# Forty fixed steps of attention on TensorE, two-bank logits rows and gated products over five heads

## The chip, the cores and the metric

The kernel runs on one core of one Trainium2 chip. A core has five engines with instruction streams of their own: TensorE (PE in the profile, with its weight loads shown apart as PEld), VectorE (DVE), ScalarE (ACT), GpSimd (POOL) and SyncE (SP, which here only issues DMA transfers). They share an on-chip memory of 128 partitions and an accumulator memory, PSUM, of eight banks of 128 x 512 float32 into which TensorE writes. The engines run side by side and wait for each other through semaphores; each executes its own stream in order.

The metric is the device time of one execution in microseconds, as the median over runs. Lower is better.

## The reference, cut to what matters

One layer of a decoder block over 1024 tokens of width 1024, in float32. Attention with 8 heads of 64 and a gated mixer of 512 channels stand side by side, and a convolutional feed-forward network follows.

```python
xn = rmsnorm(h, norm_mix_g)
proj = xn @ w_in                       # q, k, v, u, vg, forget gates
# attention, per head, per block of 128 queries
c = cumsum(log_sigmoid(forget + b_forget))
logits = q @ k.T * Dh ** -0.5 + c_q - c_k
p = softmax(where(causal, logits, -inf))
att = p @ v
# gated mixer
sg = u * (tril(w_spatial) @ rmsnorm(vg) + b_spatial)
h = h + concat([att, sg]) @ w_out
h = h + conv_ffn(rmsnorm(h), ...)      # 1024 -> 2 x 2816 -> 1024
out = rmsnorm(h, norm_final_g)
```

The change concerns the attention of the eight heads and the product of the gated mixer's result with its half of `w_out`, which the kernel computes during attention.

## The kernel before, in words

Matrix products are made in a split format: each operand is held as a rounded high part and the remainder, a low part, so that one product becomes two or three matmuls (high x high, high x low, low x high). The high part is a copy that rounds, the low part a subtraction.

The program has stages: the input projection; the gated mixer, whose result is turned by transposes on TensorE into `sgT` (`turn_sg`); attention; the out-projection of the attention half (`wmm`, lines 963 to 965) with the second normalisation; the feed-forward network (lines 1054 and 1306); the final normalisation. A planner orders the instructions of each engine from their dependencies and the order in which the program lists them; ordering edges that carry no semaphore are put in by hand with `after(...)`.

**Attention** is `att_head(h)`, called for h = 0 to 7. It loads q and k of the head in split form (tiles A, B, B2), and `ck`, a row of cumulative gates broadcast over the partitions. Then it runs over four pairs i = 0 to 3 of query blocks, two blocks j = 2i and 2i+1 of 128 queries each:

- Logits row j covers the keys 0 to (j+1) x 128, in one or two pieces of at most 512 columns, each in a PSUM bank of its own (tag "s", four banks). Each piece is two matmuls (L783, L784).
- The causal mask is written by POOL (`affine_select`, L776): it reads `ck` and writes the masked columns of the last piece to the row's own tile.
- DVE reduces each piece (L786): it adds the gates, stores the result and takes the running minimum; where a row has two pieces, the second starts from the minimum of the first. Each is followed by a read of the accumulator. A head has 12 of these.
- ACT takes the exponential of the whole row and sums it (L789).
- For each pair of key blocks (k0) a group follows: TensorE transposes the probabilities (L812) into a bank of tag "b", ACT copies the high part (L813, tile `pt`), DVE subtracts the low part (L814), and TensorE multiplies with the values (L822) into another bank. A head has 10 groups.
- After the pairs 1 and 3, ACT and DVE evacuate the finished half (L828, L829) to `attF`.

`row_tail(h)` inverts the row sums and transposes them (L730), and sends them through memory to be spread over the columns; it is called in the next head at i = 0. `pair_end` multiplies a finished pair of heads by these and splits the product in high and low (L744, L747, L750), on POOL for the first three pairs, behind the last select of pair i = 2 in head 2, 4 or 6. `wo_load` brings the attention half of `w_out`; POOL splits it (L873, L874).

**The fills.** `sg_out` is a generator: each step computes one 128 x 512 tile of the gated mixer's product with its half of `w_out`, in 12 matmuls (L851 to L853), an addition of the input on DVE (L854) and a store. There are 16 steps. The list `FILLS` says how many steps are listed behind each pair i of each head: one and two in turn, so that all 16 are listed by the third pair of head 2. The weights of the second half of the columns are split on ACT and POOL (L153, L159) ahead of the ninth step.

PSUM is one pool for the whole program: four banks of tag "s" and four of tag "b" (transposes, values, fills, row tails).

Of the kernel before, what the change touches and what calls it, by code (L numbers as in the profile page):

```python
# [8 lines left out]
F32 = mybir.dt.float32  # L9
# [3 lines left out]
ALU = mybir.AluOpType  # L13
# [6 lines left out]
FILLS = [1, 2] * 10 + [2] + [0] * 11  # L20
# [44 lines left out]
def block_kernel(ctx: ExitStack, tc: tile.TileContext, xT, xtok, wuv, wv, wqk, wf, cpk, bfv,  # L65
# [12 lines left out]
    psa = ctx.enter_context(tc.tile_pool(name="psa", bufs=4, space=bass.MemoryType.PSUM))  # L78
# [645 lines left out]
    def row_tail(h, ex):  # L724
# [5 lines left out]
        pe.transpose(ptr[0:8, 0:P], rs, ident)  # L730
        c = act.copy(rt, ptr[0:8, 0:P])
        if ex is not None:
            after(tc, c, ex)
# [4 lines left out]
    def pair_end(p, sel):  # L738

        attT[p] = sb("A" if p < 2 else "G", [P, 2, 1024], F32R)  # L740
        f = attF[p]
        for o in (slice(0, 512), slice(512, 1024)):
            eng = pool if p < 3 else dve
            m = eng.tensor_tensor(out=f[:, 0, o], in0=f[:, 0, o], in1=f[:, 1, o], op=ALU.mult)  # L744
            if p < 3:
                after(tc, m, sel)
                pool.tensor_copy(attT[p][:, 0, o], f[:, 0, o])  # L747
            else:
                act.copy(attT[p][:, 0, o], f[:, 0, o])
            eng.tensor_tensor(out=attT[p][:, 1, o], in0=f[:, 0, o], in1=f32(attT[p][:, 0, o]), op=ALU.subtract)  # L750

    def att_head(h, order=(0, 1, 2, 3)):
        p, hh = h // 2, h % 2
        ab, nb = sb("x1", [P, 2, 1024], F32R), sb("x2", [P, 2, 1024], F32R)
        A, B, ck, B2 = ab[:, 0, :], ab[:, 1, :], f32(nb[:, 0, :]), nb[:, 1, :]
        sp.dma_start(out=f32(A), in_=qd[h].rearrange("s d t -> (s d) t"))
        sp.dma_start(out=f32(B), in_=kd[h].rearrange("s d t -> (s d) t"))
        sp.dma_start(out=ck, in_=ncd[h:h + 1, :].to_broadcast((P, 1024)))
        sp.dma_start(out=f32(B2[0:64, :]), in_=kd[h, 1])
        loads[h] = sp.dma_start(out=f32(B2[64:128, :]), in_=kd[h, 0])  # L760
        if hh == 0:
            attF[p] = sb("H", [P, 2, 1024])
        rs = sml.tile([P, 8], F32, tag="rs", name=nm("rs"))
        rows[h] = rs
        po = None
        for i in order:
            w1, w2 = (2 * i + 1) * P, (2 * i + 2) * P
            tp = sb(TTAG[i][h % 2], [P, w1 + w2])
            tj = (tp[:, 0:w1], tp[:, w1:w1 + w2])
            for jj in range(2):  # L770
                j = 2 * i + jj
                n = (j + 1) * P
                qs = slice(j * P, (j + 1) * P)
                t = tj[jj]
                c0 = (j // 4) * 512
                sel = pool.affine_select(out=t[:, c0:n], in_=ck[:, c0:n], pattern=[[-1, n - c0]], compare_op=ALU.is_ge,  # L776
                                   fill=BIG, base=j * P - c0, channel_multiplier=1)
                mn = sml.tile([P, 2], F32, tag="mn", name=nm("mn"))
                lo_ = lim[:, 0:1]
                for c in range(0, n, 512):  # L780
                    e = min(n, c + 512)
                    ps = sbank()
                    pe.matmul(ps[:, 0:e - c], A[:, qs], B[:, c:e], start=True, stop=False)  # L783
                    pe.matmul(ps[:, 0:e - c], A[:, qs], B2[:, c:e], start=False, stop=True)  # L784
                    m = mn[:, c // 512:c // 512 + 1]
                    dve.tensor_tensor_reduce(out=t[:, c:e], in0=ps[:, 0:e - c], in1=(t if c == c0 else ck)[:, c:e], scale=1.0,  # L786
                                             scalar=lo_, op0=ALU.add, op1=ALU.min, accum_out=m)
                    lo_ = m
                ex = act.activation(t, t, AF.Exp, bias=lo_, scale=-1.0, accum_out=rs[:, j:j + 1])  # L789
                exs.append(ex)  # L790
            sels[h].append(sel)
            if h == 7 and i == 3:
                wo_load((2, 3))
                row_tail(7, None)
            if h > 0 and i == 0:
                row_tail(h - 1, ex)
            if h in (2, 4, 6) and i == 2:
                pair_end(p - 1, sel)
            for _ in range(FILL[4 * h + list(order).index(i)]):
                next(filler, None)  # L800
            if i % 2 == 0:
                po = bank()
            oc = (i % 2) * 256
            for k0 in range(0, 2 * i + 2, 2):
                pt = sb("pt", [P, 2, 512], F32R)
                ptr = bank()
                diag = k0 == 2 * i
                blocks = [(k0, 0, 0), (k0, 1, 128)] + ([(k0 + 1, 1, 256)] if diag else
                                                      [(k0 + 1, 0, 256), (k0 + 1, 1, 384)])
                w = 384 if diag else 512  # L810
                for k, jj, c in blocks:
                    pe.transpose(ptr[:, c:c + P], tj[jj][:, k * P:(k + 1) * P], ident)  # L812
                act.copy(pt[:, 0, 0:w], ptr[:, 0:w])  # L813
                dve.tensor_tensor(out=pt[:, 1, 0:w], in0=ptr[:, 0:w], in1=f32(pt[:, 0, 0:w]), op=ALU.subtract)  # L814
                for k in (k0, k0 + 1):
                    lhs = V[k // 2][:, k % 2, h, :, :].rearrange("p s d -> p (s d)")
                    half = k == 2 * i + 1
                    o = (k - k0) * 256
                    n = 128 if half else 256
                    oo = oc + (128 if half else 0)  # L820
                    for s in range(2):
                        pe.matmul(po[:, oo:oo + n], lhs, pt[:, s, o:o + n], start=(k == 0 and s == 0),  # L822
                                  stop=(s == 1 and half))
            if i % 2 == 1:
                hf = i // 2
                o = slice(hf * 512, hf * 512 + 512)
                r = slice(hh * 64, hh * 64 + 64)
                act.copy(attF[p][r, 0, o], po[64:128, :])  # L828
                dve.tensor_tensor(out=attF[p][r, 0, o], in0=po[0:64, :], in1=attF[p][r, 0, o], op=ALU.add)  # L829
        if h == 7:  # L830
            pair_end(3, None)

    def sg_out():
        for hf in range(2):
            o = slice(hf * 512, hf * 512 + 512)
            whs = []
            for kp in range(2):
                wr = sb("raw", [P, 2, 512])
                sp.dma_start(out=wr, in_=wos[hf, kp])
                for j in range(2):  # L840
                    w = sb("whl", [P, 2, 512], F32R)
                    split_w(wr[:, j, :], (w[:, 0], w[:, 1]), "act", "pool")
                    whs.append(w)
            for tt in range(8):
                ts_ = slice(tt * P, (tt + 1) * P)
                hs = sb("raw", [P, 512])
                sp.dma_start(out=hs, in_=xtok[ts_, o])
                ps = fbank()
                for k in range(4):
                    w = whs[k]  # L850
                    pe.matmul(ps, sgT[k][:, 0, ts_], w[:, 0, :], start=(k == 0), stop=False)  # L851
                    pe.matmul(ps, sgT[k][:, 0, ts_], w[:, 1, :], start=False, stop=False)  # L852
                    pe.matmul(ps, sgT[k][:, 1, ts_], w[:, 0, :], start=False, stop=(k == 3))  # L853
                dve.tensor_tensor(out=hs, in0=ps, in1=hs, op=ALU.add)  # L854
                sp.dma_start(out=hpd[tt, :, o], in_=hs)
                yield
# [5 lines left out]
    def wo_load(ks):  # L862
        for k in ks:
            wr = sb("raw", [P, 1024])
            after(tc, sp.dma_start(out=wr, in_=woa[k]), loads[4])
# [5 lines left out]
            for hf in range(2):  # L871
                src = wr[:, hf * 512:hf * 512 + 512]
                after(tc, pool.tensor_copy(w[hf][:, 0], src), sels[5][2 * k + hf] if k < 2 else sels[7][3])  # L873
# [3 lines left out]
    for h in range(8):  # L877
        if h == 7:
            for _ in filler:
                pass  # L880
            wo_load((0, 1))
        att_head(h)
# [7 lines left out]
    early.release()  # L890
    upl = tc.alloc_tile_pool(name="upl", bufs=1, reuse_waits="tile")
# [513 lines left out]
    raws.release()  # L1405

# [45 lines left out]
```

## Time and profile before

| | us |
|---|---|
| median of 3 runs | 1077.31 (1076.47 to 1077.58) |
| profiled execution | 1076.71 |
| its span in the trace | 1075.0 |
| first fill matmul | 225.00 |
| last fill matmul | 304.28 |
| last value matmul of head 7 | 390.8 |
| first matmul of the feed-forward network | 437.36 |

The profile is one execution: a page with busy time by engine, the span in 40 slices, the chain of work that ended last, and groups of instructions by line; the trace behind it answers for any window. A row of a group reads: line, engine, operation, output <- inputs, shape, count | busy us, mean ns of one | idle time of the engine just before these, and what ended it. A matmul's record is longer than the time until the next one starts, so records overlap. Line numbers here are those of the kernel before unless the text says otherwise.

### The profile page before, as it was taken

How to read it: one execution, taken by the hardware profiler on the slowest of the kernel's cores; microseconds unless marked ns; L12 is line 12 of the kernel's file. 1: busy time of each engine (PE TensorE's matmuls, PEld its weight loads, DVE VectorE, ACT ScalarE, POOL GpSimd, SP SyncE). 2: the span in 40 equal slices, each digit the busy share in tenths (PEclk: the TensorE clock that was granted, in tenths of full speed). 3: DMA queues.
4: the chain of work that ended last, by engine and by line, in shares of the span. 5: the costliest groups of instructions: out<-in, count | busy, mean ns of one | idle time of the engine just before them, and what ended most of it. 6: DMA issues, size and time to landing. Idle time of an engine off the chain costs nothing.

```text
span 1075.0 us, 14470 instructions
## 1 busy us (share of the span) xinstructions
PE 1062.7 (99%) x5013; PEld 876.6 (82%) x5013; DVE 892.4 (83%) x1363; ACT 568.0 (53%) x984; POOL 249.5 (23%) x223
## 2 busy tenths in 40 slices
PE   9999999999999999999999999999999999999997
PEld 7888788787888888878888888888888888888886
DVE  5985798775689969999899999989988776898774
ACT  6666644554468855764444444444444444454653
POOL 0002134233046541054333333333322000000000
PEclk9999999999999999999999999999999999999999
DMA  9242267937557445132244513222331899433442
GB/s 345 90 140 96 74 156 218 278 118 224 188 166 207 129 137 185 72 117 98 98 137 164 170 69 127 98 98 98 108 118 45 289 326 317 125 95 97 141 125 96
DMA packets 66297, 160.80 MB, mean 150 GB/s; under 512 B 7976, under 2 KB 8240, under 8 KB 66224
## 3 DMA queue, kind: packets, MB, share of 16 engines
q1 hardware_dynamic: 65792, 159.32, 45.4%
q8 instruction: 39, 0.64, 0.2%
q10 hardware_dynamic: 432, 0.57, 0.1%
q14 instruction: 34, 0.28, 0.1%
HBM read 117.06 MB, written 42.80 MB: 149 GB/s over the span
## 4 chain that ended last, share of the span: by engine, by line
PE 77%; ACT 2%; DVE 2%; issue 1%; POOL 0%; DMA 0%; DVEq 0%; ACTq 0%
PE k L1306 19%; PE qa L1054 11%; PE qc L1054 11%; PE qd L1054 11%; PE qb L1054 5%; PE pb L822 3%; PE pb L812 2%; PE ps L257 2%; PE pf L852 1%; PE pf L853 1%; PE pf L851 1%; PE ps L783 1%; PE ps L784 1%; PE pb L964 1%; PE pb L963 1%; PE pb L965 1%
## 5 line engine op out<-in xcount | busy, mean ns | idle before, releaser
L1306 PE MATMUL k<-whb,wha 128*128 128x512 f32 x924 | 209.7, 389 | 0.0
L1306 PEld LDWEIGHTS k<-whb,wha 128*128 128x128 f32 x924 | 173.3, 188 | 36.2 <-DVE wha L159 0.2
L1054 PE MATMUL qc<-xT,whb 128*128 128x512 f32 x540 | 129.8, 389 | 0.0
L1054 PE MATMUL qa<-xB,wha 128*128 128x512 f32 x528 | 127.2, 390 | 0.0
L1054 PEld LDWEIGHTS qc<-xT,whb 128*128 128x128 f32 x540 | 101.3, 188 | 21.2 <-ACT whb L153 0.2
L1054 PEld LDWEIGHTS qa<-xB,wha 128*128 128x128 f32 x528 | 98.8, 188 | 20.8 <-DVE wha L159 0.4
L153 ACT CAST wha<-sg 128x512 fp32r<-128x512 f32 x77 | 47.8, 622 | 96.9 <-PE k L1306 85.8
L153 ACT CAST whb<-sg 128x512 fp32r<-128x512 f32 x82 | 50.5, 617 | 86.6 <-PE qc L1054 67.0
L159 DVE TENSOR_TENSOR wha<-sg,wha 128x512 fp32r<-128x512 f32 x77 | 52.7, 687 | 41.1 <-ACT wha L153 41.0
L1054 PE MATMUL qd<-xB,whb 128*128 128x512 f32 x264 | 63.9, 389 | 0.5 <-DVE h L1173 0.5
L1054 PE MATMUL qd<-xT,whb 128*128 128x512 f32 x264 | 63.6, 389 | 0.0
L159 DVE TENSOR_TENSOR whb<-sg,whb 128x512 fp32r<-128x512 f32 x82 | 58.2, 710 | 4.4 <-ACT whb L153 4.3
L941 POOL TENSOR_TENSOR sg<-raw 128x512 f32<-128x512 f32 x20 | 30.7, 1535 | 134.0 <-DVE whb L159 75.7
L813 ACT CAST pt<-pb 128x512 fp32r<-128x512 f32 (+1 forms) x80 | 40.6, 543 | 38.5 <-PE pb L812 37.4
L1054 PE MATMUL qb<-xT,whb 128*128 128x512 f32 x252 | 60.9, 389 | 0.0
L822 PE MATMUL pb<-pt,V 128*128 128x256 f32 (+1 forms) x320 | 58.7, 298 | 1.6 <-ACT pt L813 1.2
L1054 PEld LDWEIGHTS qd<-xB,whb 128*128 128x128 f32 x264 | 49.5, 188 | 11.2 <-issue 0.9
L1054 PEld LDWEIGHTS qd<-xT,whb 128*128 128x128 f32 x264 | 49.6, 188 | 10.3
L822 PEld LDWEIGHTS pb<-pt,V 128*128 128x128 f32 x320 | 46.8, 188 | 13.5 <-ACT pt L813 8.9
L1054 PEld LDWEIGHTS qb<-xT,whb 128*128 128x128 f32 x252 | 47.3, 188 | 9.8
L814 DVE TENSOR_TENSOR pt<-pb,pt 128x512 fp32r<-128x512 f32 (+1 forms) x80 | 48.1, 632 | 8.0 <-ACT pt L813 7.4
L944 POOL TENSOR_TENSOR sg<-sg,raw 128x512 f32<-128x512 f32 x20 | 33.3, 1666 | 64.6 <-DVE whb L159 64.6
(399 smaller groups left out, 2306.9 us busy)
## 6 DMA issues: line engine op xcount, KB each, us to landing
raw<-wup SPq DMA_DIRECT2D x44, 512.0 KB, 3.5
sg<-hx SPq DMA_DIRECT2D x77, 256.0 KB, 2.8
hx<-hs SPq DMA_DIRECT2D x44, 256.0 KB, 3.7
hx<-ca SPq DMA_DIRECT2D x35, 256.0 KB, 2.0
xT<-wdn SPq DMA_DIRECT2D x28, 256.0 KB, 4.1
raw<-wqk SPq DMA_DIRECT2D x8, 512.0 KB, 4.7
qd<-G SPq DMA_DIRECT2D x16, 256.0 KB, 3.9
kd<-G SPq DMA_DIRECT2D x16, 256.0 KB, 3.3
```

The lines of the kernel that those rows point to most:

```text
L153: act.copy(h, src)
L159: return eng.tensor_tensor(out=l, in0=src, in1=f32(h), op=ALU.subtract)
L257: pe.matmul(banks[m], xs(n, xi, k)[:, ms], w[:, wi, :], start=(first and k == 0 and c == 0), stop=(k == 3 and c == 2), skip_group_check=True)
L783: pe.matmul(ps[:, 0:e - c], A[:, qs], B[:, c:e], start=True, stop=False)
L812: pe.transpose(ptr[:, c:c + P], tj[jj][:, k * P:(k + 1) * P], ident)
L813: act.copy(pt[:, 0, 0:w], ptr[:, 0:w])
L814: dve.tensor_tensor(out=pt[:, 1, 0:w], in0=ptr[:, 0:w], in1=f32(pt[:, 0, 0:w]), op=ALU.subtract)
L822: pe.matmul(po[:, oo:oo + n], lhs, pt[:, s, o:o + n], start=(k == 0 and s == 0), stop=(s == 1 and half))
L941: pool.tensor_tensor(out=s[0], in0=a21, in1=a22, op=ALU.add)
L944: pool.tensor_tensor(out=s[3], in0=s[1], in1=a12, op=ALU.add)
L1054: pe.matmul(ps, w[:, wi, ks], xb[:, xi, k, :], start=(first and n == 0), stop=(n == 11), skip_group_check=True)
L1306: pe.matmul(banks[bk + m], xh[:, xi, ms], wh[:, wi, :], start=(first and p_ == 0 and n == 0), stop=(p_ == NP - 1 and n == 2), skip_group_c ...
```

## The change

Attention is written anew as a sequence that fixes the order of every TensorE instruction of the stage (`seq` chains each to the one before).

- There are 40 steps, five for each head, each with two of the head's ten groups, pairs i in the order 3, 2, 1, 0. `turn_p` (transposes, cast, low part) of the next step is issued ahead of `values` of this one.
- The logits of head h+1 are issued during head h, behind the values of a step: rows 7; 6; 5; 4 and 3; 2, 1 and 0. Those of head 0 come first, in a prologue.
- A logits row lies in one tile of 1024 columns, two neighbouring banks (tag "L", two such tiles). DVE reduces the whole row in one instruction (L797 of the changed file), 8 per head.
- The mask is written in place: POOL's select (L789) changes the 128 columns of the diagonal block in `ck` itself, one per row, from row 7 down.
- A value group multiplies first the two high parts, then the two low parts.
- `row_tail(h)` comes in step 1 of head h. `pair_half` (one half of a pair's product) stands in step 2 of heads 2, 4 and 6, both halves, on POOL behind the select of row 6 of the next head.
- The fills: one step each after rows 4, 2 and 0 of the prologue, then after steps 0, 2 and 4 of heads 0, 2 and 4 and steps 1 and 3 of heads 1 and 3. The second half's weights are loaded at the seventh step and split behind the eighth.
- All four parts of the attention half of `w_out` are loaded behind head 6's loads; POOL splits two behind selects of head 6 (which fall in head 5) and two behind select 4 of head 7 (which falls in head 6). The changed lines are L897 and L898.
- PSUM is taken as three pools in turn (before, during and after attention).

```diff
-FILLS = [1, 2] * 10 + [2] + [0] * 11
+FILLS = {(-1, j): 1 for j in (4, 2, 0)} | {(h, s): 1 for h in range(5) for s in ((0, 2, 4), (1, 3))[h % 2]}
...
+    def pair_half(p, o):
...
+        m = eng.tensor_tensor(out=f[:, 0, o], in0=f[:, 0, o], in1=f[:, 1, o], op=ALU.mult)
+        if p < 3:
+            after(tc, m, sels[2 * p + 3][1])
+            pool.tensor_copy(attT[p][:, 0, o], f[:, 0, o])
...
+        eng.tensor_tensor(out=attT[p][:, 1, o], in0=f[:, 0, o], in1=f32(attT[p][:, 0, o]), op=ALU.subtract)
+    psa.release()
+    psa = tc.alloc_tile_pool(name="psb", bufs=4, space=bass.MemoryType.PSUM, reuse_waits="tile")
+    def seq(m):
+        if order:
+            after(tc, m, order[0])
+        order[:] = [m]
+    cks, b2s = sb("x2", [P, 2, 1024]), sb("x2", [P, 2, 1024], F32R)
...
+    def logits(h, j):
...
+        sels[h].append(pool.affine_select(out=ck[:, qs], in_=ck[:, qs], pattern=[[-1, P]], compare_op=ALU.is_ge,
+                                          fill=BIG, base=0, channel_multiplier=1))
+        mn = sml.tile([P, 1], F32, tag="mn", name=nm("mn"))
+        ps = psa.tile([P, 1024], F32, tag="L", bufs=2, name=nm("pl"))
+        for c in range(0, n, 512):
+            e = min(n, c + 512)
+            seq(pe.matmul(ps[:, c:e], A[:, qs], B[:, c:e], start=True, stop=False))
+            seq(pe.matmul(ps[:, c:e], A[:, qs], B2[:, c:e], start=False, stop=True))
+        dve.tensor_tensor_reduce(out=t, in0=ps[:, 0:n], in1=ck[:, 0:n], scale=1.0, scalar=lim[:, 0:1],
+                                 op0=ALU.add, op1=ALU.min, accum_out=mn)
+        exs.append(act.activation(t, t, AF.Exp, bias=mn, scale=-1.0, accum_out=rows[h][:, j:j + 1]))
+    def turn_p(g):
...
+        for k, jj, c in blocks:
+            seq(pe.transpose(ptr[:, c:c + P], tj[jj][:, k * P:(k + 1) * P], ident))
+        act.copy(pt[:, 0, 0:w], ptr[:, 0:w])
+        dve.tensor_tensor(out=pt[:, 1, 0:w], in0=ptr[:, 0:w], in1=f32(pt[:, 0, 0:w]), op=ALU.subtract)
+        return pt
+    def values(g, pt):
...
+        for s in range(2):
+            for k in (k0, k0 + 1):
...
+                seq(pe.matmul(po[0][:, oo:oo + n], lhs, pt[:, s, o:o + n], start=(k == 0 and s == 0),
+                              stop=(s == 1 and half)))
...
-            after(tc, sp.dma_start(out=wr, in_=woa[k]), loads[4])
+            after(tc, sp.dma_start(out=wr, in_=woa[k]), loads[6])
...
-                after(tc, pool.tensor_copy(w[hf][:, 0], src), sels[5][2 * k + hf] if k < 2 else sels[7][3])
+                after(tc, pool.tensor_copy(w[hf][:, 0], src), sels[6][2 * k + hf] if k < 2 else sels[7][3])
...
+    STEPS = [[(h, i, 2 * c) for i in (3, 2, 1, 0) for c in range(i + 1)] for h in range(8)]
+    STEPS = [s[n:n + 2] for s in STEPS for n in range(0, 10, 2)]
+    NEXT = ((7,), (6,), (5,), (4, 3), (2, 1, 0))
...
+    for j in range(7, -1, -1):
+        logits(0, j)
+        fill((-1, j))
+    turned = [turn_p(g) for g in STEPS[0]]
+    for n, step in enumerate(STEPS):
+        h, s = n // 5, n % 5
+        if s == 0 and h < 6:
+            head_loads(h + 2)
+        if h == 7 and s == 0:
...
+            wo_load((0, 1))
+            wo_load((2, 3))
+        if s == 1:
...
+            row_tail(h)
+        if h in (2, 4, 6) and s == 2:
+            for o in (slice(0, 512), slice(512, 1024)):
+                pair_half(h // 2 - 1, o)
+        now, turned = turned, [turn_p(g) for g in STEPS[n + 1]] if n + 1 < len(STEPS) else []
+        for g, pt in zip(step, now):
+            values(g, pt)
+        if h < 7:
+            for j in NEXT[s]:
+                logits(h + 1, j)
+        fill((h, s))
...
     early.release()
+    psa.release()
+    psa = tc.alloc_tile_pool(name="psc", bufs=4, space=bass.MemoryType.PSUM, reuse_waits="tile")
```

More of the change, by code (lines that the diff above doesn't have):

```diff
@@ L77, in block_kernel @@
     FTAG, FB, BB = FCFG
-    psa = ctx.enter_context(tc.tile_pool(name="psa", bufs=4, space=bass.MemoryType.PSUM))
+    psa = tc.alloc_tile_pool(name="psa", bufs=4, space=bass.MemoryType.PSUM)
     uid = [0]
@@ L729, in row_tail @@
         dve.reciprocal(rs, rs)
[L730 to L733, printed above, removed]
+        seq(pe.transpose(ptr[0:8, 0:P], rs, ident))
+        act.copy(rt, ptr[0:8, 0:P])
         act.dma_start(out=rsd[h], in_=rt)
@@ L736, in row_tail @@
                      in_=rsd[h].rearrange("a b -> (a b)").unsqueeze(0).to_broadcast((64, 1024)))
-    def pair_end(p, sel):
-        attT[p] = sb("A" if p < 2 else "G", [P, 2, 1024], F32R)
+    def pair_half(p, o):
+        if attT[p] is None:
+            attT[p] = sb("A" if p < 2 else "G", [P, 2, 1024], F32R)
         f = attF[p]
[L742 to L831, printed above, removed]
@@ new lines, in block_kernel, with head_loads @@
+    order = []
+    def seq(m):
[3 more added lines that the diff above has]
+    cks, b2s = sb("x2", [P, 2, 1024]), sb("x2", [P, 2, 1024], F32R)
+    abs_, places = [None] * 8, {}
+    def head_loads(h):
+        ab = sb("x1", [P, 2, 1024], F32R)
+        abs_[h] = ab
+        hh = h % 2
+        sp.dma_start(out=f32(ab[:, 0, :]), in_=qd[h].rearrange("s d t -> (s d) t"))
+        sp.dma_start(out=f32(ab[:, 1, :]), in_=kd[h].rearrange("s d t -> (s d) t"))
+        sp.dma_start(out=cks[:, hh, :], in_=ncd[h:h + 1, :].to_broadcast((P, 1024)))
+        sp.dma_start(out=f32(b2s[0:64, hh, :]), in_=kd[h, 1])
+        loads[h] = sp.dma_start(out=f32(b2s[64:128, hh, :]), in_=kd[h, 0])
+        rows[h] = sml.tile([P, 8], F32, tag="rs", name=nm("rs"))
@@ new lines, in turn_p @@
+    def turn_p(g):
+        h, i, k0 = g
+        tj = places[h, i]
+        ptr = bank()
+        pt = sb("pt", [P, 2, 512], F32R)
+        diag = k0 == 2 * i
+        blocks = [(k0, 0, 0), (k0, 1, 128)] + ([(k0 + 1, 1, 256)] if diag else
+                                              [(k0 + 1, 0, 256), (k0 + 1, 1, 384)])
+        w = 384 if diag else 512
+        for k, jj, c in blocks:
[3 more added lines that the diff above has]
+        return pt
@@ new lines, in block_kernel @@
+    po = [None]
+    def values(g, pt):
+        h, i, k0 = g
+        if i % 2 == 1 and k0 == 0:
+            po[0] = bank()
+        oc = (i % 2) * 256
+        for s in range(2):
+            for k in (k0, k0 + 1):
+                lhs = V[k // 2][:, k % 2, h, :, :].rearrange("p s d -> p (s d)")
+                half = k == 2 * i + 1
+                o = (k - k0) * 256
+                n = 128 if half else 256
+                oo = oc + (128 if half else 0)
+                seq(pe.matmul(po[0][:, oo:oo + n], lhs, pt[:, s, o:o + n], start=(k == 0 and s == 0),
+                              stop=(s == 1 and half)))
+        if i % 2 == 0 and k0 == 2 * i:
+            p, hh = h // 2, h % 2
+            o = slice((i // 2) * 512, (i // 2) * 512 + 512)
+            r = slice(hh * 64, hh * 64 + 64)
+            if attF[p] is None:
+                attF[p] = sb("H", [P, 2, 1024])
+            act.copy(attF[p][r, 0, o], po[0][64:128, :])
+            dve.tensor_tensor(out=attF[p][r, 0, o], in0=po[0][0:64, :], in1=attF[p][r, 0, o], op=ALU.add)
+            if h == 7:
+                pair_half(3, o)
@@ L833, in sg_out, with load @@
     def sg_out():
-        for hf in range(2):
-            o = slice(hf * 512, hf * 512 + 512)
-            whs = []
+        def load(hf):
+            wrs = []
             for kp in range(2):
@@ L839, in sg_out, with split @@
                 sp.dma_start(out=wr, in_=wos[hf, kp])
[L840 to L843, printed above, removed]
+                wrs += [wr[:, 0, :], wr[:, 1, :]]
+            return wrs
+        def split(wrs, lo_eng):
+            whs = []
+            for wr in wrs:
+                w = sb("whl", [P, 2, 512], F32R)
+                split_w(wr, (w[:, 0], w[:, 1]), "act", lo_eng)
+                whs.append(w)
+            return whs
+        whs = split(load(0), "pool")
+        for hf in range(2):
+            o = slice(hf * 512, hf * 512 + 512)
             for tt in range(8):
+                if hf == 0 and tt == 6:
+                    nxt = load(1)
                 ts_ = slice(tt * P, (tt + 1) * P)
@@ L850, in sg_out @@
                     w = whs[k]
-                    pe.matmul(ps, sgT[k][:, 0, ts_], w[:, 0, :], start=(k == 0), stop=False)
-                    pe.matmul(ps, sgT[k][:, 0, ts_], w[:, 1, :], start=False, stop=False)
-                    pe.matmul(ps, sgT[k][:, 1, ts_], w[:, 0, :], start=False, stop=(k == 3))
+                    seq(pe.matmul(ps, sgT[k][:, 0, ts_], w[:, 0, :], start=(k == 0), stop=False))
+                    seq(pe.matmul(ps, sgT[k][:, 0, ts_], w[:, 1, :], start=False, stop=False))
+                    seq(pe.matmul(ps, sgT[k][:, 1, ts_], w[:, 0, :], start=False, stop=(k == 3)))
                 dve.tensor_tensor(out=hs, in0=ps, in1=hs, op=ALU.add)
                 sp.dma_start(out=hpd[tt, :, o], in_=hs)
+                if hf == 0 and tt == 7:
+                    whs = split(nxt, "pool")
                 yield
@@ L1405, in block_kernel @@
     raws.release()
+    psa.release()
 def layouts(inp):
```

24 lines of the change are left out of this document (20 added, 4 removed).

## The prediction

> **What bounds the kernel now.** I read the page's first lines, then stage sums, then the waits of the attention stage.
>
> ```profile
> span 1075.0 us, 14470 instructions
> PE 1062.7 (99%) x5013; PEld 876.6 (82%) x5013; DVE 892.4 (83%) x1363; ACT 568.0 (53%) x984; POOL 249.5 (23%) x223
> ...
> PE 77%; ACT 2%; DVE 2%; issue 1%; POOL 0%; DMA 0%; DVEq 0%; ACTq 0%
> ...
> L1306 PE MATMUL k<-whb,wha 128*128 128x512 f32 x924 | 209.7, 389 | 0.0
> ```
>
> TensorE is called 99% busy and carries 77% of the chain, but a matmul's record is longer than its slot: L1306 lasts 389 ns, and 209.7 us / 924 = 0.227 us is its pace. So "busy" hides loss, and I count slots. The stage sums (columns: window, length, then busy us and count of PE, weight loads, DVE, ACT, POOL; granted clock; DMA):
>
> ```profile
> 226.00:305.00 79.00, 78.23 (x425) 63.69 (x424) 46.03 (x112) 35.94 (x79) 19.44 (x30) 1.00 0.51 164
> 305.00:391.00 86.00, 84.17 (x584) 73.70 (x581) 76.84 (x202) 69.77 (x159) 40.01 (x60) 1.00 0.56 171
> 391.00:405.00 14.00, 14.00 (x64) 11.62 (x63) 8.44 (x10) 4.01 (x7) 8.20 (x6) 1.00 0.37 139
> 405.00:435.00 30.00, 30.00 (x158) 24.89 (x157) 28.77 (x47) 19.25 (x41) 3.08 (x3) 1.00 0.59 211
> 1060.00:1075.00 15.00, 8.08 (x36) 6.37 (x34) 6.14 (x12) 6.53 (x16) 0.00 (x0) 0.85 0.34 140
> 225.00:391.03 166.03, 163.43 (x1010) 138.28 (x1010) 123.86 (x314) 106.68 (x240) 60.45 (x92) 1.00 0.53 167
> ```
>
> The change lives in 225.0 to 391.0. From TensorE's timeline (start, length, count in a run), the first and last fill matmul, runs of value matmuls and transposes, and the first and last out-projection matmul inside the stage:
>
> ```profile
> 225.00 0.50 PE L851 MATMUL pf<-whl,G 128*128 128x512 f32 x1
> 304.28 0.39 PE L853 MATMUL pf<-whl,G 128*128 128x512 f32 x1
> 339.93 0.93 PE L822 MATMUL pb<-pt,V 128*128 128x256 f32 x7
> 340.69 1.39 PE L812 MATMUL pb<-ident,t 128*128 128x128 f32 x11
> L963 PE MATMUL ps<-whl,A x3: 390/394/478, 379.5 to 384.6; 128*128 128x512 f32 x3
> 390.98 0.45 PE L964 MATMUL pb<-whl,A 128*128 128x512 f32 x1
> ```
>
> Paces: 256 wide (340.69 - 339.93) / 7 = 0.11 us, a transpose about 1.25 / 11 = 0.114. A head holds 24 logits matmuls (12 of 512, 4 each of 384, 256, 128: 4.1 us), 36 transposes (4.1), 32 value matmuls of 256 and 8 of 128 (4.1): 12.3 us, eight heads 98.4. Of this 1.1 us (logits) ran before 225.0. Fills: 16 x 12 x 0.227 = 43.6; 17 out-projection matmuls 3.9. Dense sum 97.3 + 43.6 + 3.9 = 144.8 of 166.0: **21.2 us are lost**. At 305 the fills have run out in head 2, and 5.4 heads are to go: 5.4 x 12.3 + 3.9 = 70.3 of 86.0, so 15.7 of the loss lies there, with DVE busy 76.84. What waits:
>
> ```profile
> PEld pb L822 <- ACT pt L813: 8.9, 31, 0.6
> PE pb L822 <- ACT pt L813: 1.2, 4, 0.4
> ```
>
> The casts hold the value matmuls 31 times, never above 0.6 us. From 391.0 on the out-projection is lossless (14.00 of 14.00, 30.00 of 30.00): whatever moves the end of attention, corrected for the out-projection done by then, moves the end of the kernel.
>
> **The change, part by part.** Without stalls, attention from 225.0 would take 98.4 + 43.6 = 142.0 us; out-projection matmuls now stand behind the last value matmul in the fixed order, so the 3.9 us done early before are still due. Against 391.0 the new mark is 225.0 + 142.0 + 3.9 + S = 370.9 + S, with S the stalls: **even at S = 20.1**. So I need S.
>
> *Durations for the vector chain:*
>
> ```profile
> L786 DVE CUSTOM_DVE_ANT_0 gg<-ps,gg,lim 128x128 f32<-128x128 f32 x8 | 2.7, 341 | 0.0
> L786 DVE CUSTOM_DVE_ANT_0 t<-ps,x,lim 128x512 f32<-128x512 f32 x16 | 11.8, 744 | 0.2 <-PE ps L784 0.2
> L786 DVE DVE_READ_ACCUMULATOR2_ANT mn<- 128x1 f32 x96 | 7.8, 81 | 0.0
> L814 DVE TENSOR_TENSOR pt<-pb,pt 128x512 fp32r<-128x512 f32 x48 | 32.0, 686 | 5.3 <-ACT pt L813 4.8
> 226.66 0.33 DVE L786 CUSTOM_DVE_ANT_0 gg<-ps,gg,lim 128x128 f32<-128x128 f32 x1
> 331.77 0.49 DVE L786 CUSTOM_DVE_ANT_0 t<-ps,t,mn 128x256 f32<-128x256 f32 x1 [0.17 <-POOL gg L776]
> ```
>
> A reduce grows by (744 - 341) / 3 = 134 ns per 128 columns. A 1024-wide one does not occur here. Bounds: two 512-wide ones, 2 x (0.74 + 0.08) = 1.64, and one alone, 0.82; I take the line, 0.34 + 7 x 0.134 + 0.08 = 1.36, since the measured widths lie on it. One reduce per row in place of up to two saves DVE about 1.1 us a head. A POOL result reaches DVE 0.17 us later.
>
> *The mask in place.* The select on `ck` (L789 of the changed file) must wait for the reduce of the row above (it read the unmasked columns), and its own reduce waits for the select: DVE, POOL, DVE in series down the rows. Two `L` tiles mean logits j wait for reduce j+2. POOL's rows:
>
> ```profile
> 330.96 0.65 POOL L776 TENSOR_SCALAR_AFFINE_SELECT gg<-x 128x128 f32<-128x128 f32 x2 [11.14 <-ACT t L789]
> 368.48 2.54 POOL L744 TENSOR_TENSOR H<-H 128x512 f32<-128x512 f32 x2 [5.90 <-DMA H<-rsd]
> 370.96 1.17 POOL L747 CAST G<-H 128x512 fp32r<-128x512 f32 x2
> 372.09 2.54 POOL L750 TENSOR_TENSOR G<-H,G 128x512 fp32r<-128x512 f32 x2
> ...
> 375.15 1.17 POOL L873 CAST G<-raw 128x512 fp32r<-128x512 f32 x2
> 376.28 2.53 POOL L874 TENSOR_TENSOR G<-raw,G 128x512 fp32r<-128x512 f32 x2
> ...
> L159 POOL TENSOR_TENSOR whl<-raw,whl x7: 1292/1297/1307, 215.3 to 265.2; 128x512 fp32r<-128x512 f32 x7
> ```
>
> A select is 0.33. In the last steps of a head logits 4 to 0 follow closely. From the end of logits 4: reduce 4 takes 1.0, select 3 with its hand-off 0.5, reduce 3 1.0, two low-part subtractions ahead on DVE 1.4, reduce 2 0.8: 4.7 us before logits 0 may start, against 2.5 us of TensorE work (logits 3, 2, 1, eight transposes, eight value matmuls): 2.2 us stall. Even heads have their fill behind it (uncovered); odd heads have one ahead (0.8 left).
>
> *Prologue.* DVE is free only at 226.66, so reduce 7 ends at 228.0, logits 5 and 4 of head 0 wait 1.4 + 0.9 = 2.3; a fill then covers the rest.
>
> *Heads 0 to 4:* 3 x 2.2 + 2 x 0.8 + 0.6 (head 2 opens behind the second half's weight splits, 1.3 us each, which sit between selects on POOL) = 8.8. The pair products of heads 2 and 4 (2.54 + 1.17 + 2.54 = 6.2 us on POOL, between selects 6 and 5) lie under two fills of 2.7. Without those they would cost what head 6 shows.
>
> *Head 5*, no fill: 2.2, plus 0.9 for four copies and subtractions (1.8 each) of out-projection weights between its selects, plus 0.6 since DVE needs about 13 us to TensorE's 12.3: 3.7. Before, heads without fills took (391 - 305) / 5.4 = 16 us; this gives 12.3 + 3.7 = 16.0.
>
> *Head 6* is where the change is dearest. POOL's order there is select 6, both pair halves (6.2), select 5, select 4, three casts and two subtractions of weights 2 and 3 (4.3), select 3, the other 3.1, selects 2, 1, 0. From the end of logits 7: reduce 7 and hand-off 1.5, select 6 0.5, pair 6.2 (8.2), select 5 and reduce 5 1.6 (9.8), select 4 0.3 and 4.3 of weights (14.4), select 3 and reduce 3 1.4 (15.8; POOL's 3.1 run alongside, 17.8), select 2 and reduce 2 1.2: logits 0 start at about 19. TensorE has 9.7 us of work there: **9.3 us lost**, as stalls of about 2, 3.4 and 3.1 us before logits 3, 1 and 0. In the kernel before, masks go to a fresh tile, need no reduce, and run ahead (the 330.96 select waits for a buffer), so the same POOL work held nobody.
>
> *Head 7* has no logits: only the cast and low-part chain, one step ahead, and nothing to slip in. Between nothing and five steps of the longest cast wait, 5 x 0.6 = 3.0; I take 1.9, nearer the upper end since no logits cover it.
>
> S = 2.3 + 8.8 + 3.7 + 9.3 + 1.9 = 26.0, so 26.0 - 20.1 = **+5.9 us**. On the profiled execution's 1076.71 us: 1082.6; the median of the three runs is 0.6 above that execution, hence 1083.2, say 1083.0.
>
> *Costed at nothing:* the row tail one head earlier, the two weight loads behind a later load on SP's queue (they land heads before POOL reads them; if late, POOL's order only shifts further into head 6), the PSUM pools' release (the new pool's tiles wait for tiles long read), and fewer bank switches. What it removes that cost before, the 8.9 + 1.2 us of cast waits, is inside the 21.2.
>
> *The clock.* The stages show 1.00 wherever TensorE never stands, and 0.85 in the tail, where it is busy 8.08 of 15.00. The Trainium skill, "TensorE: Matmul & The Clock Gate", section "What's actually happening", says an idle window of about 3.4 us halves the clock until it has been busy for as long again. Head 6's stalls are of that size; by that rule two of them would add an estimated 1.7 us each. The tail's row agrees in direction; no row of the stage can show it, and the sum has none of it.
>
> **Rivals.**
> (a) *Faster: the head-6 chain doesn't bind and the step-ahead turn removes the cast waits.* For it: 10.1 us of those waits, and fills spread over stalls that ran bare after 305. It needs head 6 at 2, half the last-step stalls: S = 2.3 + 4.4 + 2.5 + 2 + 1.5 = 12.7, -7.4: 1070. Against: POOL's rows in head 6 sum to 13.6 us beside the selects, more than a head of TensorE.
> (b) *No change:* only head 6 is misjudged (it behaves as head 5 does, less its copies: 3): S = 19.7, 1077.
> (c) *Slower, by the clock:* the tail's row lost 0.15 x 15 = 2.25 us of clock around one long idle. If each 3 us stall of head 6 does that, two add 4.5: 1087.5. Against: no idle of that length before the tail exists to judge by. By the Trainium skill's rule above it would be an estimated 1086.5.
> (d) *Much slower: the fixed order exposes every hand-off.* With nothing to slip in, heads 0 to 4 lose as much as head 5 (5 x 3.7 = 18.5 for 8.8): 1092.7. For it: 31 small cast waits that other work filled. Against: the turn one step ahead, and 2.7 us of fill in most steps.
>
> **Chances.** Forecast 0.48, (a) 0.19, (b) 0.11, (c) 0.10, (d) 0.12. Within 0.2% (2 us) is about what this kernel's measurement can't tell from no change. Slower 0.70, same 0.11, faster 0.19. The range goes from 1071, within (a), to 1092, just short of (d); the forecast's own is 1079 to 1087, with S off by 4 either way.
>
> **What would show it.** Right: in head 6, idle TensorE ahead of L795 put down to the reduce (L797), DVE idle before L797 put down to the select (L789), POOL solid in L743 to L749 and L897/L898; the last value matmul (L831) near 393 with L1021 straight behind; fills (L873) to about 345. Wrong: head 6 at 16 us or less (b), last L831 before 385 (a), a clock under 1.00 in the stage (c), idle of 3 to 4 us in each of heads 0 to 4 (d).

## The result and the profile after

The changed kernel takes 1095.95 us (median of five runs, 1094.35 to 1099.69) against 1077.31: a ratio of 1.0176, 95% interval 1.0157 to 1.0194. It is 18.6 us slower; the forecast was 5.9 us slower, and the time lies above the stated range. The profiled execution, 1099.69 us, is the slowest of the five, so its trace shows more loss than the median has.

The page of the changed kernel, the lines that answer to those of before:

```profile
span 1097.9 us, 14436 instructions
PE 1066.0 (97%) x5013; PEld 884.7 (81%) x5013; DVE 892.3 (81%) x1299; ACT 572.5 (52%) x984; POOL 240.2 (22%) x223
...
PE 66%; issue 8%; DVE 4%; POOL 3%; DMA 3%; ACT 1%; SPq 0%; POOLq 0%; ACTq 0%; DVEq 0%
...
L1364 PE MATMUL k<-whb,wha 128*128 128x512 f32 x924 | 209.7, 389 | 0.0
```

The last stage (L1364, before L1306) costs the same 209.7 us, and TensorE's share of the chain falls from 77% to 66%. The stage sums (columns as before) and the run of value matmuls, with their first and last start:

```profile
225.00:409.70 184.70, 164.29 (x1002) 144.57 (x1001) 123.27 (x251) 111.86 (x241) 56.69 (x101) 0.94 0.48 151
409.70:459.60 49.90, 49.90 (x248) 41.34 (x248) 39.73 (x60) 24.81 (x50) 11.27 (x8) 1.00 0.48 169
```

```profile
L831 PE MATMUL pb<-pt,V x320: 220/282/562, 243.8 to 409.5; 128*128 128x256 f32 x160
```

Attention ends at 409.7 where it ended at 391.0, and the out-projection behind it is lossless (49.90 of 49.90). 18.7 later, plus 3.9 us of out-projection no longer done early, is 22.6: nearly the whole difference of the spans (22.9).

In the prediction's formula, 225.0 + 142.0 + S = 409.7, so S was 42.7 and not 26.0. The row splits it: TensorE idle 184.70 - 164.29 = 20.4; clock, at a mean of 0.94 (rounded, so to about 1 us), 0.06 x 184.7 = 11.1; the remaining 11.2 is hidden loss, the part in which TensorE counts as busy but not at its pace. The same split of before: idle 166.03 - 163.43 = 2.6, clock nothing, hidden 21.2 - 2.6 = 18.6.

What ended the idle, from the waits of the stage (total, times, longest):

```profile
PE pl L795 <- DVE mn L797: 18.8, 11, 3.4
PE pb L831 <- DVE pt L814: 1.4, 3, 0.7
```

And what the idle does to the clock, around the end of head 1: a row of TensorE's timeline, then windows with columns as before.

```profile
290.02 0.33 PE L795 MATMUL pl<-x 128*128 128x128 f32 x1 [3.41 <-DVE mn L797]
```

```profile
286.00:290.00 4.00, 0.61 (x4) 0.40 (x3) 2.60 (x5) 2.32 (x6) 2.49 (x3) 1.00 0.50 154
291.00:294.60 3.60, 3.60 (x16) 3.21 (x15) 1.72 (x6) 1.85 (x6) 0.23 (x1) 0.54 0.93 275
295.00:305.00 10.00, 10.00 (x62) 8.71 (x61) 6.18 (x11) 5.79 (x11) 7.19 (x10) 1.00 0.68 200
```

Soon after TensorE resumes (1.3 us here, 0.1 to 1.5 us in the other cases), its clock is granted at half rate for 3.4 us, while it is fully busy (3.60 of 3.60). There are six such dips in the stage, the last one of 6.8 us and partly idle; three of them:

```profile
230.00:233.80 3.80, 3.80 (x11) 3.13 (x12) 1.92 (x4) 2.97 (x6) 0.80 (x3) 0.57 0.00 0
264.00:267.80 3.80, 3.80 (x11) 2.98 (x10) 0.87 (x5) 1.15 (x5) 0.29 (x1) 0.55 0.77 267
397.00:403.50 6.50, 4.59 (x22) 4.53 (x23) 3.43 (x10) 3.66 (x10) 1.78 (x4) 0.51 0.23 82
```

In the trace the six begin at 229.87, 264.00, 291.31, 335.68, 376.64 and 397.12 us: 10, 8, 13, 12 and 6 times 3.41 us apart. So it looks as if the clock changes only at the ends of fixed steps of 3.41 us, wherever the stall lies; that is an inference from these starts.

### The profile page after: what moved, and what is told of

Its sections match the earlier page's. It is cut to its first block, busy times and chain, and to the rows that moved or that the text cites. A ratio compares the mean times of both kernels' runs of the same rounds, so it can differ in the third digit from the quotient of the medians.

```text
span 1097.9 us, 14436 instructions
## 1 busy us (share of the span) xinstructions
PE 1066.0 (97%) x5013; PEld 884.7 (81%) x5013; DVE 892.3 (81%) x1299; ACT 572.5 (52%) x984; POOL 240.2 (22%) x223
## 4 chain that ended last, share of the span: by engine, by line
PE 66%; issue 8%; DVE 4%; POOL 3%; DMA 3%; ACT 1%; SPq 0%; POOLq 0%; ACTq 0%; DVEq 0%
PE k L1364 19%; PE qa L1112 11%; PE qc L1112 10%; PE qd L1112 10%; PE qb L1112 5%; PE pb L831 1%; PE pb L1021 1%; PE pb L812 1%; PE pb L1023 1%; PE pb L1022 1%; DMA raw<-wos 1%; POOL x L789 1%; DVE G L44 1%; PE ps L258 1%; DMA x<-kd 1%
## 5 line engine op out<-in xcount | busy, mean ns | idle before, releaser
L1364 PE MATMUL k<-whb,wha 128*128 128x512 f32 x924 | 209.7, 389 | 0.0
L1364 PEld LDWEIGHTS k<-whb,wha 128*128 128x128 f32 x924 | 173.3, 188 | 36.2 <-DVE wha L160 0.2
L813 ACT CAST pt<-pb 128x512 fp32r<-128x512 f32 (+1 forms) x80 | 42.7, 540 | 30.6 <-PE pb L812 24.7
L1112 PEld LDWEIGHTS qd<-xB,whb 128*128 128x128 f32 x264 | 49.5, 188 | 11.2 <-issue 0.9
L795 PE MATMUL pl<-x 128*128 128x512 f32 (+1 forms) x96 | 36.0, 378 | 19.0 <-DVE mn L797 18.8
L831 PE MATMUL pb<-pt,V 128*128 128x256 f32 x320 | 50.2, 302 | 1.4 <-DVE pt L814 1.4
L789 POOL TENSOR_SCALAR_AFFINE_SELECT x<-x 128x128 f32<-128x128 f32 x64 | 18.6, 293 | 142.0 <-DVE mn L797 96.0
```

Source lines behind the costliest of these rows:

```text
L789: sels[h].append(pool.affine_select(out=ck[:, qs], in_=ck[:, qs], pattern=[[-1, P]], compare_op=ALU.is_ge, fill=BIG, base=0, channel_multi ...
L795: seq(pe.matmul(ps[:, c:e], A[:, qs], B[:, c:e], start=True, stop=False))
L831: seq(pe.matmul(po[0][:, oo:oo + n], lhs, pt[:, s, o:o + n], start=(k == 0 and s == 0), stop=(s == 1 and half)))
L1112: pe.matmul(ps, w[:, wi, ks], xb[:, xi, k, :], start=(first and n == 0), stop=(n == 11), skip_group_check=True)
L1364: pe.matmul(banks[bk + m], xh[:, xi, ms], wh[:, wi, :], start=(first and p_ == 0 and n == 0), stop=(p_ == NP - 1 and n == 2), skip_group_c ...
```

## The experiments

There were two theories at first: the serial chain from reduce to select to reduce opens the stalls and the clock falls behind them (1), or the fixed order of TensorE exposes waits that the planner had filled (2). Medians below stand against 1095.95 of the changed kernel, which was not timed again beside them, and 1077.1 to 1077.7 of the kernel before in the same jobs. In brackets: the ratio to the kernel before, with its 95% interval; the changed kernel's is 1.0176 (1.0157 to 1.0194).

**The mask on TensorE.**

```diff
-        sels[h].append(pool.affine_select(out=ck[:, qs], ...))
+        seq(pe.matmul(ps[:, j * P:n], identb, maskb, start=False, stop=True))
```

> The changed kernel with the causal mask added on TensorE: one more 128 wide matmul (identity times a mask of zeros and 3e38) per logits row in place of POOL's select on the gates, so that no reduce waits for POOL and no select for a reduce. It adds 64 x 0.057 = 3.6 us of TensorE work. Theory 1 (the serial chain reduce, select, reduce opens the stalls, and each stall then costs clock): idle TensorE ahead of L795 falls from 19.0 us to under 6, the clock lost in the stage from 12 us to under 4, so 1096 - 13 - 8 + 3.6 = about 1078 (1073 to 1083). Theory 2 (the fixed order itself exposes the waits for the reduces): the stalls stay, 1094 to 1100.

1085.76 us (1.0081, 1.0066 to 1.0096). The idle ahead of the logits fell from 18.8 to 8.9 and the clock recovered but for one place, so theory 1 holds for about half of the idle and most of the clock; the time stayed above the 1078 expected (1073 to 1083).

```profile
PE pl L796 <- DVE mn L800: 8.9, 8, 3.0
```

The largest part of what is left is one stall of 3.0 us at the end of head 1, with no select anywhere. In the kernel of this run, the timeline of ACT and of TensorE there, and a window:

```profile
281.58 1.65 ACT L154 CAST whl<-raw 128x512 fp32r<-128x512 f32 x3
283.25 1.07 ACT L816 CAST pt<-pb 128x512 fp32r<-128x512 f32 x2
...
286.58 0.48 PE L796 MATMUL pl<-x 128*128 128x128 f32 x1 [3.03 <-DVE mn L800]
```

```profile
285.00:292.00 7.00, 5.42 (x22) 4.82 (x22) 3.68 (x11) 2.76 (x8) 7.00 (x7) 0.53 0.66 209
```

The half rate begins at 285.37 here, while TensorE still stands, and lasts 6.8 us. ACT casts the fill weights of the second half ahead of two probability casts; DVE's subtractions, the evacuation and then the reduces come late behind them. Stalls of 1.29 and 1.22 us at the ends of heads 5 and 6 are left too; ahead of the first, DVE works from 362.6 to 370.9 us without a gap of over 0.1 us, so that one is DVE's own work and not POOL's.

**Empty work in the stalls.** 70 matmuls that nobody reads, then 43:

```diff
+        for _ in range(WARMUPS.get((h, j), 0)):
+            seq(pe.matmul(ps[:, 512:1024], A[:, qs], B[:, 0:512], start=True, stop=True))
```

> The changed kernel with idle filled by empty work: matmuls of 512 columns whose result nobody reads, into a bank that is free, behind the logits rows after which the trace shows TensorE idle (5 to 14 of them at 0.227 us each, as many as fit the idle measured there, 70 in all). Nothing else moves. Theory 1: the idle comes back as clock: the granted clock of 0.50 for some 3.4 us behind six of the stalls stays at 1.00, and 9 to 11 us are gained: 1085 to 1087, with less useless TensorE work than time gained. Rival (the clock costs nothing, since DVE and POOL set the pace in those stretches): 1094 to 1099.

> The kernel of e2_warm with 43 empty matmuls in place of 70 (9.8 us in place of 15.9), so that none can lengthen a stall. If it was their length that ate the gain of e2, the clock still stays at 1.00 and the time falls by another 1 to 3 us, to 1090 to 1092. If the lost clock is worth no more than e2 showed: 1092 to 1094. If the shorter filling lets the clock fall again: 1094 or more.

1093.06 us (1.0155, 1.0138 to 1.0172) and 1091.86 us (1.0131, 1.0115 to 1.0146). The first lies between its two ranges, and its interval overlaps the changed kernel's; the second is clear of it. The second's stage:

```profile
225.00:402.00 177.00, 164.99 (x1047) 142.67 (x1045) 122.75 (x251) 111.71 (x241) 57.08 (x102) 1.00 0.49 158
```

The clock is 1.00 throughout (in the first run too), although 9.8 us of useless work were added and TensorE still idles 12.0 us, in gaps of at most 1.3. So the dips follow from the idle and cost time by themselves: 4.1 us in the medians, and 1097.9 - 1090.3 = 7.6 between the two profiled spans, of 11.1 us of clock in the trace. Part of the difference is the execution that was profiled: it was granted 0.987 over its span, the other four of the changed kernel 0.990 to 0.994. An estimate of the clock lost in the stage, (1 - clock) x span less 2.2 us for the tail (0.15 x 15), gives 12 us for the profiled one and 4 to 9 for the others. That the rest fell where TensorE would have waited anyway is likely (of the last dip's 6.50 us, 1.9 are idle) but not shown. The first run's expectation (1085 to 1087) took all of the profiled clock loss for a gain and was wrong.

**The planner's order**, the rest unchanged:

```diff
-        if order:
-            after(tc, m, order[0])
         order[:] = [m]
```

> The changed kernel without the chain over TensorE's instructions: the planner orders them by its own costs; all else stays. Theory 1 (the chain through POOL and DVE makes the stalls): the planner can pull transposes and values ahead of a waiting logits row in some places, but the chain is as long: 1086 to 1096, and head 6 still idle before L795. Theory 2 (the fixed order makes the stalls): 1077 or less.

1084.56 us (1.0073, 1.0058 to 1.0088): 11.4 us gained, just beyond theory 1's range and far from theory 2's. The idle ahead of the logits falls to 5.8 us although the chain through POOL stays:

```profile
PE pl L793 <- DVE mn L795: 5.8, 9, 2.7
```

Both theories held a part, and the parts overlap.

**Out-projection weights later**, so that they leave head 6:

```diff
-  ... sels[6][2 * k + hf] if k < 2 else sels[7][3])
+  ... sels[6][2 * k + hf] if k < 2 else sels[7][7])
```

> The changed kernel with one word changed: the split of the out-projection weights 2 and 3 on POOL (7.4 us) waits for the last select of head 7 instead of the fourth, so it no longer stands between selects of head 6. Theory 1 (POOL's queue in head 6): of the idle 1.0 + 2.65 + 2.75 us ahead of logits 3, 1 and 0 some 1.5 to 2.5 stay, and the clock dip behind them goes or shrinks: 5 to 7 us gained, 1089 to 1091. Rival (the reduces alone hold logits there): 1094 to 1098.

1094.54 us (1.0163, 1.0147 to 1.0178). In head 6 the stall ahead of logits 1 went from 2.65 to 0.15 us and that ahead of logits 0 from 2.75 to 1.28, as the queue on POOL would have it, and the last two of the six dips are gone. Yet the median is only 1.4 us lower, in the rival's range, and the intervals overlap: no gain is shown. Other waits came (0.67 us ahead of the last row tail; 1.47 in place of 0.67 ahead of a value matmul in head 5). And all four executions here were granted 0.993, as much as the changed kernel's outside its profiled one (0.990 to 0.994), so its median may not have had all six dips either.

**The casts off ACT**, on top of the first run:

```diff
-                    whs = split(nxt, "pool")
+                    whs = split(nxt, "pool", "pool")
```

> The kernel of e1_mask_on_pe with one thing more: the split of the second half of the fill weights has its four casts on POOL, where ACT had them ahead of two probability casts. Theory: the idle of 3.0 us at the end of head 1 and the clock lost behind it (2.7 us) come from ACT's order alone and go: 1085.8 - 5.7 = 1080 (1078 to 1082). Rival (the reduce on DVE sets that stall): 1084 to 1087.

1081.6 us (1.0042, 1.0027 to 1.0057): 4.2 gained. The 3.03 us stall is 0.69 there, and no dip is left in the stage.

**Low rows masked in a fresh tile**, as the kernel before did; nothing added to TensorE:

```diff
+        if j < 4:
+            g = t
+            sels[h].append(pool.affine_select(out=t, in_=ck[:, 0:n], pattern=[[-1, n]], ... base=j * P, ...))
```

> The changed kernel with the mask of rows 3 to 0 written to a fresh tile, as in the kernel before; rows 7 to 4 stay masked in place. So in the last steps of a head no select waits for a reduce, and TensorE has no extra work. Theory 1 (serial chain): the idle of 1.2 to 1.8 us ahead of logits 0 in heads 0, 2, 3, 4 and 5 goes, that of head 1 (3.4) and head 6 (2.65 + 2.75) stays in part, since POOL's and ACT's weight splits still stand ahead; the clock dips fall from six to two or three: 1096 - 8 - 4 = 1084 (1081 to 1088). Rival (DVE's order, not POOL's answer, holds the reduces): 1093 to 1097.

1085.47 us (1.0084, 1.0066 to 1.0102). This is theory 1 without another change of work, as forecast (1084):

```profile
PE pl L801 <- DVE mn L803: 12.1, 11, 3.1
```

The stalls of 1.23 us at the ends of heads 0, 2 and 4 shrink to 0.50, and in head 6 those of 2.65 and 2.75 to 0.16 and 1.28; two dips stay of six. But the ends of heads 1, 3 and 5 keep 3.06, 1.45 and 1.23 (from 3.41, 1.79 and 1.24), where heads 3 and 5 were forecast to lose theirs: there it was not POOL's answer that held TensorE.

**The spread of the fills alone**, in the kernel before:

```diff
-FILLS = [1, 2] * 10 + [2] + [0] * 11
+FILLS = [1, 1, 1, 0, 1] * 4 + [0] * 12
```

> The kernel before with its fills alone spread over five heads: one behind each of the first, second, third and fifth pair in turn, in place of 16 by head 2. Theory 1 (fills cover what is lost in heads without them): of the 15.7 us lost after the fills ran out, heads 3 and 4 keep theirs covered: 1070 (1068 to 1073). Theory 2 (the waits only move, since heads 5 to 7 stay bare and DVE has to carry the additions there): 1075 to 1079.

1078.0 us (1.0013, 1.0002 to 1.0024): nothing gained. DVE's load did move, since this stretch now holds five of the fills and less of the heads' work (columns as in the stage sums; before, DVE was busy 76.84 of these 86 us and TensorE idle 1.83):

```profile
305.00:391.00 86.00, 83.24 (x539) 70.81 (x538) 67.88 (x173) 60.94 (x136) 36.78 (x52) 1.00 0.50 157
```

DVE has 9 us less to do there, and TensorE idles 2.76 us; attention ends no earlier. So a lighter DVE in that stretch did not by itself make the stage shorter.

**The planner's order with the mask on TensorE and the casts on POOL.**

> The kernel of e5_mask_pe_split_pool without the chain over TensorE's instructions. Theory 1 (fixed order and in-place mask hurt by the same stalls): no better than e5, 1079 to 1083. Theory 2 (they hurt apart: the fixed order also exposes the small waits for casts): 1072 to 1077.

1076.82 us (0.9996, 0.9987 to 1.0006): 4.8 us under the same kernel in fixed order. Once the chain is gone, the fixed order by itself costs that much. The other parts of the change (wide rows, steps, spread fills, order of the products) together pay for the mask matmuls, since the time is that of the kernel before; the runs do not take them apart.

**Variants of it.** Half of the mask matmuls back to POOL (rows 3 to 0, fresh tile); two fills moved to head 5; and all masks on POOL in the planner's order, rows 7 to 4 in place (with the casts on POOL, and out-projection weights 2 and 3 behind the last select):

```diff
+        if j < 4:
+            g = t                       # select on POOL, as above
+        else:
+            seq(pe.matmul(ps[:, j * P:n], identb, maskb, start=False, stop=True))
```

> The kernel of e8_free_mask_pe (planner's order, mask on TensorE, casts of the fill weights on POOL) with the mask of rows 3 to 0 back on POOL, into a fresh tile: half of the 64 mask matmuls (32 x 0.057 = 1.8 us) go, and no wait comes in their place if the fresh tile is free early. Theory: 1076.8 - 1.8 = 1075 (1074 to 1076). Rival (POOL's splits stand ahead of the selects in heads 5 and 6): 1077 to 1080.

> The kernel of e9_mixed_mask with two of the fills moved from heads 0 and 4 to head 5. Theory 1 (a head without fills loses about 3 us, as heads 5 to 7 do in the traces, since DVE needs more than TensorE there): 1 to 2 us better than e9. Theory 2 (spreading does nothing by itself, as e7 showed): the same within 1 us; and worse by 1 to 3 if the weights of the out-projection, which wait for the last fill, come late.

> The changed kernel with four edits: planner's order, rows 3 to 0 masked into a fresh tile, casts of the second half's fill weights on POOL, out-projection weights 2 and 3 split behind the last select. No work is added to TensorE; rows 7 to 4 keep the mask in place. Theory: with the serial chain gone from the last steps and ACT's and POOL's splits out of the way, 1073 to 1076. Rival (rows 7 to 4 still hold DVE for POOL, above all in head 6 behind the pair products): 1078 to 1082.

1075.03 us (0.9974, 0.9964 to 0.9985), 1075.19 us (0.9977, 0.9967 to 0.9986) and 1079.66 us (1.0018, 1.0009 to 1.0026). The first is 0.26% under the kernel before. Its stage and the out-projection behind it:

```profile
225.00:383.50 158.50, 156.29 (x1027) 135.43 (x1025) 119.64 (x250) 106.24 (x236) 51.88 (x68) 1.00 0.55 177
383.50:433.40 49.90, 49.90 (x248) 41.41 (x247) 39.70 (x60) 24.37 (x50) 11.27 (x8) 1.00 0.46 169
```

Idle is 2.2 us, the clock 1.00, and the stage ends at 384 in place of 409.7. Where the fills go makes no difference again. In the third, the chain through POOL returns in head 6: the select of row 5 (371.36) stands behind the pair products, and that of row 4 (376.33) behind weight splits, since the last select, behind which these were put, now runs early. The reduces wait for both selects, and TensorE for what DVE does behind them. The timelines of POOL, DVE and TensorE:

```profile
368.90 2.51 POOL L749 TENSOR_TENSOR G<-H,G 128x512 fp32r<-128x512 f32 x2
371.36 0.30 POOL L793 TENSOR_SCALAR_AFFINE_SELECT x<-x 128x128 f32<-128x128 f32 x1
371.61 1.17 POOL L901 CAST G<-raw 128x512 fp32r<-128x512 f32 x2
372.74 2.54 POOL L902 TENSOR_TENSOR G<-raw,G 128x512 fp32r<-128x512 f32 x2
375.21 1.18 POOL L901 CAST G<-raw 128x512 fp32r<-128x512 f32 x2
376.33 0.31 POOL L793 TENSOR_SCALAR_AFFINE_SELECT x<-x 128x128 f32<-128x128 f32 x1
```

```profile
371.70 1.02 DVE L801 CUSTOM_DVE_ANT_0 H<-pl,x,lim 128x768 f32<-128x768 f32 x1 [3.46 <-POOL x L793]
...
376.68 0.88 DVE L801 CUSTOM_DVE_ANT_0 H<-pl,x,lim 128x640 f32<-128x640 f32 x1 [2.42 <-POOL x L793]
```

```profile
372.78 0.50 PE L799 MATMUL pl<-x 128*128 128x512 f32 x1 [2.73 <-DVE mn L801]
...
378.09 1.12 PE L816 MATMUL pb<-ident,H 128*128 128x128 f32 x4 [2.44 <-DVE pt L818]
```

## Why the prediction was right and wrong

- **The frame held; the direction was partly luck.** Attention's end sets the kernel's end, the out-projection behind it is dense, and the serial chain through POOL is a large cause: the mask on TensorE takes 10.2 us off although it adds 3.6, and rows 3 to 0 in a fresh tile take 10.5 off. But the sum said slower because it put the stalls at 26.0. With the idle that was measured, 20.4, it gives 20.4 - 20.1 = 0.3 us: no change. The loss grew from 21.2 to 42.7 us: idle by 17.8, clock by 11.1, hidden loss down by 7.4.
- **The failed step: "even at S = 20.1".** The 21.2 us of before were counted in slots, so they held 18.6 of hidden loss. S was summed from named stalls alone. Measured like for like, the changed kernel has hidden loss of 11.2 beside its idle. With a term of that size, S would have been 37 and the forecast about 1094, with the stalls 5.6 too high in place of the clock. One part of it went as planned: the waits of weight loads for casts (8.9 us, 31 times) are no longer among the waits of the stage. What the remaining 11.2 consist of is not shown.
- **The failed step: the clock, "and the sum has none of it".** The row of the tail spoke against that, and rival (c) had the mechanism with two dips at 2.25 us. There were six, 11.1 us of clock in the profiled execution, worth 4.1 in the medians by the run with 43 empty matmuls. The rule of the Trainium skill, "TensorE: Matmul & The Clock Gate", section "What's actually happening", was right on the half rate and its length (0.50 for some 3.4 us). Its idle of about a window is not needed here: 1.23 us was enough at 263.4, and not at 312.2 and 357.7.
- **The terms of S, as visible idle.** Prologue 2.3: 2.2. Heads 0, 2 and 4, 2.2 each: 1.23 each; select and reduces did as the chain says, but the subtractions ran in the wait for POOL. Head 5, 3.7: 1.9. Head 6, 9.3 in stalls of 2, 3.4 and 3.1: 1.03, 2.65 and 2.75 (and 0.5), in those places. Head 7, 1.9: nothing visible. Head 1, 0.8 and 0.6 for the splits: 3.41; only POOL's part was priced, and ACT's casts ahead of the probability casts were the cause, as the casts moved to POOL showed (4.2 us). Head 3, 0.8: 1.79. So heads 0 to 4 sum to 8.9 against 8.8, by luck: the errors cancel.
- **The POOL rows of head 6** came out nearly as laid down: select 6, then the pair products, and at last select 2, with the pair halves and the weights between them. The timeline of POOL, then of TensorE:

```profile
382.33 0.29 POOL L789 TENSOR_SCALAR_AFFINE_SELECT x<-x 128x128 f32<-128x128 f32 x1 [4.54 <-DVE mn L797]
382.60 2.54 POOL L743 TENSOR_TENSOR H<-H 128x512 f32<-128x512 f32 x2
...
397.90 0.29 POOL L789 TENSOR_SCALAR_AFFINE_SELECT x<-x 128x128 f32<-128x128 f32 x1
```

```profile
395.65 0.38 PE L795 MATMUL pl<-x 128*128 128x256 f32 x1 [2.65 <-DVE mn L797]
398.91 0.47 PE L795 MATMUL pl<-x 128*128 128x128 f32 x1 [2.75 <-DVE mn L797]
```

- **Durations.** The 1024-wide reduce, 1.36 with its read, took 1.28 + 0.08: the line through the narrower ones held.

```profile
L797 DVE CUSTOM_DVE_ANT_0 H<-pl,x,lim 128x1024 f32<-128x1024 f32 x4 | 5.1, 1284 | 2.8 <-PE pl L796 2.8
```

- **Rival (d)**, that the fixed order exposes hand-offs, was a part of it and not an alternative: 4.8 us with the chain gone, 11.4 with it there, as much as the chain's own 10 to 11. The two overlap, so their sizes don't add.
- **Left open.** How the lost clock falls into the medians run by run: 1094.35 us came with a clock of 0.992, 1095.69 with 0.994. And why equal idles of 1.23 us trip it in one place and not in another. Where the idle lies in the steps of 3.41 us can be one reason: the idle before 312.2 is cut by the end of a step at 311.8. It is not the only one, since the idle before 357.7 lies whole within a step (356.2 to 359.6) and no dip followed.

## What to carry to other kernels

Count a stage's loss in one unit before and after: slots against slots, with idle, clock and hidden loss apart. Before writing a mask in place, see whether it ties two engines into a chain that runs once per row, and what else stands in that engine's queue. An order fixed by hand needs its waits covered everywhere, since a gap of about a microsecond or more on TensorE may be paid again in clock.

## What the runs showed of the hardware

- TensorE's granted clock halves after short idle: 1.23 us (head 0, 0.55 over the next 3.8 us), and after 3.03 us in the first run, 0.53 over 7 us. Gaps of at most 1.31 us, left by the 43 empty matmuls, never tripped it, so length alone does not decide. The dips last 3.41 us or twice that, and begin whole multiples of 3.41 us apart (229.87 to 397.12).
- A 128-wide bfloat16 matmul adds a mask of 3e38 into an accumulation of two float32 matmuls; 64 of them in place of 64 selects on POOL that had to answer DVE took the time from 1095.95 to 1085.76 us.
